# Ordering merge-gate products behind attention scores in a two-layer hybrid decoder trunk

## The chip, the cores and the metric

One NeuronCore of one Trainium2 chip runs the whole program. The metric is device time in microseconds (us) of one execution; before the change it is 1164.12 us, the median of 3 runs. Lower is better.

## What is computed

The reference is a decoder trunk of two layers on 256 tokens of width 1024, all in float32. Per layer:

```python
h = rms_norm(x, norm_g[l, 0]) * (1.0 + sc1) + sh1
p = h @ w_in[l] + b_in[l]
p_rwkv, p_q, p_kv, p_gate, p_merge = jnp.split(p, IN_SPLITS, axis=-1)
...
m_a, m_b = jnp.split(jax.nn.sigmoid(p_merge), 2, axis=-1)
mix = m_a * (y_a @ w_up_rwkv[l]) + m_b * (y_b @ w_up_nsa[l])
x = x + gate_mix * (mix @ w_out[l])
h2 = rms_norm(x, norm_g[l, 1]) * (1.0 + sc2) + sh2
...
```

Between the lines shown, `y_a` comes from the recurrent heads (8 of 64 channels), `y_b` from the sparse attention (8 query heads in 2 key groups); behind them stands the mixture of 16 experts.

The change concerns `p_merge`: 2048 columns of the input projection, of which the sigmoid gates the two branches. They depend on `h` alone, on neither branch.

## The kernel before, in words

Everything lies transposed (channels on partitions, tokens along the free axis). A layer runs through these stages: input norm; projections of the recurrent heads; the recurrent branch, which for each of four pairs of heads prepares (`prep`), inverts (`inverse`) and then runs a chain of four chunks (`chain`, lines 626 to 704); the attention branch; the "up" products, where the two branches are projected and gated (lines 1077 to 1094); the output projection; routing; the experts, whose weights (about 1 MB a load, L1076) stream in through rings of buffers.

**Merge tiles.** The 2048 gate columns are done as 16 tiles of 128 columns by `merges(n)` (lines 713 to 721), which takes the next n of them each time it is called. A tile is made in four steps. ACT rounds the weights to the high half (`split`, L274), DVE makes the low half (L275), each over 128 x 1024. PE multiplies in 24 products of 128 x 256 (`mm3`, L288): for each of 8 slices of the contraction high by high, low by high and high by low. ACT takes the tanh into `mth` (L721). The two halves lie in the tags `w20` and `w21` of the pool `wsp`, which has 2 buffers for each tag, so two tiles can be held at once; the PSUM tag `mm` has 2 buffers. One 1 MB weight load (L160, `in_win`) serves two tiles and lies in a ring of 3 buffers (`ringa`), whose later users are the first three expert loads.

**Order.** The program is traced once in Python, and a list scheduler then lays out each engine's queue: what was traced earlier has priority, and what is ready sooner than its elders fills gaps. Buffers go to tiles in that order too. Each engine runs its queue strictly in the order laid out. `tc.issue_after(x)` adds the condition that what the block traces on x's engine stands behind x in that queue; nothing waits for x's result.

The recurrent and the attention work of a layer is interleaved by the list `STEPS`, which ends in "c2 c3 q1 m4 r": the last two chains, a projection, merge tiles 0 to 3, and the rotation of the queries. Behind it stands the attention proper. It first makes the zero-padded keys `KZ` (L938 on DVE, L939 on ACT), then compressed attention for two halves of the queries (L947 to L966). Then it runs over two groups g (lines 970 to 1028):

- 16 score matrices, 4 heads r for each of two query halves qt (L982, PE), which take turns in the PSUM tags `tr` and `rw`; the masked maximum of each (L985, DVE); exponentials (L991, ACT); sums and scaling (L993 to L1001, DVE);
- for hp = 0 and 1, the group's "middle": `merges(2)`, one step of the modulation vector (`ada_step`, L225 on DVE, weights by L223), transposes of the probabilities (L1012 to L1014), copies (L192, ACT), the products with the values (L1020 to L1026), and the output (L1028).

So tiles 4 to 7 are traced in group 0, 8 to 11 in group 1, and 12 to 15 behind both. The lines of the loop that the change touches:

```python
            for hp in range(2):
                merges(2)
                ada_step()
```

Of the kernel before, what the change touches and what calls it, by code (L numbers as in the profile page):

```python
# [18 lines left out]
T = 256  # L19
# [92 lines left out]
def tile_trunk(ctx: ExitStack, tc: tile.TileContext, a: dict, layers=L, dump=None):  # L112
    nc = tc.nc
    ve, ac, po, pe, sp = nc.vector, nc.scalar, nc.gpsimd, nc.tensor, nc.sync
# [17 lines left out]
    def ps(tag):  # L132
        return phase["pool"].tile([128, 512], F32, name="ps_" + tag, tag=tag, bufs=phase["bufs"][tag])
# [56 lines left out]
    def cp(e, out, x):  # L190
        if e == "a":
            ac.activation(out, x, AF.Copy)  # L192
        else:
            ENG[e].tensor_copy(out, x)
# [77 lines left out]
    def split(hi, lo, x, e=ve):  # L272

        ac.activation(hi, x, AF.Copy)  # L274
        e.tensor_sub(lo, x, hi.bitcast(F32))  # L275
# [7 lines left out]
    def mm3(out, w2, x2, ks=range(NK)):  # L283

        for j in range(2):
            for k in ks:
                for i in range(2 - j):
                    pe.matmul(out, lhsT=w2[i][:, k, :], rhs=x2[j][:, k, :], start=(k == ks[0] and not (i or j)),  # L288
                              stop=(k == ks[-1] and j == 1), skip_group_check=True)
# [8 lines left out]
    with tc.tile_pool(name="start", bufs=8, reuse_waits="tile") as start:  # L298
# [11 lines left out]
        for ci in (2, 0, 3, 1):  # L310
            p = ps("mm")
            for r in range(2):
                w = load("ada0", ci, r, pool=start)
                for j in range(4):
                    pe.matmul(p[32 * j:32 * j + 32, :], lhsT=csx[:, 4 * r + j], rhs=w[:, 512 * j:512 * j + 512],
                              start=(r == 0), stop=(r == 1), skip_group_check=True)
            rows_ = start.tile([128, 512], F32, name="adar", tag="adar", bufs=2)
            ac.activation(rows_, p, AF.Copy)
            p = ps("rw")
# [8 lines left out]
    for l in range(layers):  # L328
# [8 lines left out]
        def pair(name, pool):  # L337

            return [pool.tile([128, NK, T], F32R, name=f"{name}{i}", tag=f"{name}{i}") for i in range(2)]

        h2 = pair("h2", lay)
# [6 lines left out]
        def parts(k, n):  # L348

            return [wsp.tile([128, 1024], F32R, name=f"w2{i}", tag=f"w2{i}")[:, 0:k * n].rearrange("p (k n) -> p k n", k=k)  # L350
                    for i in range(2)]
# [29 lines left out]
        def wcol(ci, l=l, win=win):  # L381
            if ci not in win:
                win[ci] = load("win", l, ci).rearrange("p (k n) -> p k n", k=4 if 8 <= ci < 12 else NK)
            return win[ci]
# [321 lines left out]
        def ada_step():  # L706

            if todo:
                ada_piece(*todo.pop(0), crow, adp)

        merged = iter(range(16))

        def merges(n):

            for j in itertools.islice(merged, n):
                w = wcol(12 + j // 2)
                p = ps("mm")
                w2 = parts(NK, 128)
                split(*w2, w[:, :, 128 * (j % 2):128 * (j % 2) + 128])
                mm3(p[:, 0:T], w2, h2)  # L720
                ac.activation(mth[:, j, :], p[:, 0:T], AF.Tanh, scale=0.5, bias=hbm[:, j:j + 1])  # L721


        def nt(shape, name, bufs=1, dt=F32, pool=None):
            return (pool or nka).tile([128] + shape, dt, name=name, tag=name, bufs=bufs)
# [18 lines left out]
        qT = nt([4, T], "qT")  # L744
# [140 lines left out]
        for step in STEPS.split():  # L885
            n = int(step[1:]) if step[1:] else 0
# [42 lines left out]
        KZ = nt([2, 2, T], "KZ")  # L929
        PcT = nt([2, T], "PcT")  # L930
        p = ps("tr")
# [12 lines left out]
        for qt in range(2):  # L944
            p = ps("tr")
            for h in range(8):
                pe.matmul(p[:, 32 * h:32 * h + 32], lhsT=qT[:, h // 2, qt * 128:qt * 128 + 128], rhs=KCZ[:, h % 2, :],  # L947
                          start=True, stop=True)
# [21 lines left out]
        for g in range(2):  # L970
            E = []
            for qt in range(2):
                n = 128 * (qt + 1)
                S_ = nt([4, 2, n], f"S{qt}", 2)
                mx = nt([4, 2], "mx", 2)
                am = R[:, C_AM + 128:C_AM + 256] if qt == 0 else R[:, C_AM:C_AM + 256]
                for r in range(4):
                    h = 4 * g + r
                    p = ps("rw" if r % 2 else "tr")
                    p3 = p[:, 0:2 * n].rearrange("p (b k) -> p b k", b=2)  # L980
                    s = slice(64 * (h % 2), 64 * (h % 2) + 64)
                    pe.matmul(p3, lhsT=qT[s, h // 2, qt * 128:qt * 128 + 128], rhs=KZ[s, g, :, 0:n],  # L982
                              start=True, stop=True)
                    for b in range(2):
                        ve.tensor_tensor_reduce(S_[:, r, b, 0:n], p3[:, b, :], am, 1.0, NEG, op0=ALU.add, op1=ALU.max,  # L985
                                                accum_out=mx[:, r, b:b + 1])
                ve.tensor_scalar(mx, mx, -0.125, None, op0=ALU.mult)
                sm_ = nt([4, 2], "sm", 2)
                for r in range(4):
                    for b in range(2):  # L990
                        ac.activation(S_[:, r, b, 0:n], S_[:, r, b, 0:n], AF.Exp, scale=0.125, bias=mx[:, r, b:b + 1],  # L991
                                      accum_out=sm_[:, r, b:b + 1])
                ve.tensor_scalar(sm_, sm_, TINY, None, op0=ALU.max)  # L993
                ve.reciprocal(sm_, sm_)
                ve.tensor_mul(sm_, sm_, GT4[:, qt, 4 * g:4 * g + 4, 1:3])
                for r in range(4):
                    for b in range(2):
                        if K["ss"] == "a" or (K["ss"] == "x" and b):
                            ac.activation(S_[:, r, b, 0:n], S_[:, r, b, 0:n], AF.Copy, scale=sm_[:, r, b:b + 1])
                        else:  # L1000
                            ve.tensor_scalar(S_[:, r, b, 0:n], S_[:, r, b, 0:n], sm_[:, r, b:b + 1], None, op0=ALU.mult)  # L1001
                E.append(S_)
            for hp in range(2):
                merges(2)
                ada_step()
                pts = []
                for i in range(2):
                    r = 2 * hp + i
                    PT = PTs[:, 768 * i:768 * i + 768].rearrange("p (b n) -> p b n", b=2)
                    for b in range(2):  # L1010
                        p = ps("rw" if b else "tr")
                        pe.transpose(p[:, 0:128], E[0][:, r, b, 0:128], ident)  # L1012
                        pe.transpose(p[:, 128:256], E[1][:, r, b, 0:128], ident)
                        pe.transpose(p[:, 256:384], E[1][:, r, b, 128:256], ident)  # L1014
                        cp("a" if b else K["pt"], PT[:, b, :], p[:, 0:384])
                    pts.append(PT)
                po_ = ps("rc")
                for b in range(2):
                    for i in range(2):
                        pe.matmul(po_[64 * i:64 * i + 64, 0:256], lhsT=VS[:, 0, b, 64 * g:64 * g + 64],  # L1020
                                  rhs=pts[i][:, b, 0:256], start=(b == 0), stop=False, skip_group_check=True)
                    for i in range(2):
                        pe.matmul(po_[64 * i:64 * i + 64, 128:256], lhsT=VS[:, 1, b, 64 * g:64 * g + 64],
                                  rhs=pts[i][:, b, 256:384], start=False, stop=False, skip_group_check=True)
                for i in range(2):
                    pe.matmul(po_[64 * i:64 * i + 64, 0:256], lhsT=VC[:, 2 * hp + i, :], rhs=PcT[:, g, :],  # L1026
                              start=False, stop=True, skip_group_check=True)
                ac.activation(ybT[:, 2 * g + hp, :], po_[:, 0:256], AF.Copy)  # L1028
# [3 lines left out]
        while todo:  # L1032
            merges(2)
            ada_step()
# [47 lines left out]
        for j in range(NK):  # L1082
            p = ps("mm")
            w2 = [wsu.tile([128, NK, 128], F32R, name=f"w2{i}", tag=f"w2{i}") for i in range(2)]
# [24 lines left out]
        for d in range(NK):  # L1109
            pe.matmul(pL[0:16, 64:65], lhsT=rw[:, 16 * d:16 * d + 16], rhs=mod[:, 24 + d:25 + d], start=(d == 0),  # L1110
                      stop=(d == NK - 1), skip_group_check=True)
# [7 lines left out]
        for d in range(NK):  # L1119
            w = wo[d // 2]  # L1120
            p = ps("mm")
            mm3(p[:, 0:T], split_w(wsu, w[:, :, (d % 2) * 128:(d % 2) * 128 + 128], po if K["olo"] and d % K["olo"] == 2 else ve), m2)
            ve.scalar_tensor_tensor(xT[:, d, :], p[:, 0:T], gmh[:, d:d + 1], xT[:, d, :], op0=ALU.mult, op1=ALU.add)
            if d % 2:
                p = ps("tr")
# [13 lines left out]
            for tt in range(2):  # L1139
                pe.matmul(pL[:, 16 * tt:16 * tt + 16], lhsT=xT[:, d, tt * 128:tt * 128 + 128], rhs=rwg[:, d, :],  # L1140
                          start=(d == 0 and tt == 0), stop=(d == NK - 1), skip_group_check=True)
# [431 lines left out]
```

## Time and profile before

| | before |
|---|---|
| median of 3 runs | 1164.12 us (1163.97 to 1164.67) |
| the profiled execution | 1167.3 us, of which the traced span is 1165.3 us |
| PE (matmul) busy | 1051.6 us, 90% of the span |
| DVE busy | 648.6 us, 56% |
| ACT busy | 401.3 us, 34% |
| POOL busy | 135.3 us, 12% |
| DMA | 328.34 MB, mean 282 GB/s |
| attention stage, layer 0 and layer 1 | about 256 to 317 us, about 820 to 877 us |

The profile is one execution. "Busy" is the time in which an engine had an instruction in work; matmuls are pipelined, so their busy times overlap and a run of them is read by its length and count. The bracket at the end of a line of the timeline is the time for which the engine stood idle before it, and whose end it then waited for. PEclk is the granted TensorE clock as a share of full speed (2.4 GHz); its two levels are 1.2 and 2.4 GHz, so 0.80 means that part of the stretch ran at the lower one.

### The profile page before, as it was taken

The page shows a single profiled execution, that of the slowest core. Times are in us where ns is not written, and L with a number is a line of the kernel's source. Part 1 is how long each engine was busy: PE and PEld are TensorE (multiplying, and loading weights), DVE is VectorE, ACT ScalarE, POOL GpSimd, SP SyncE. Part 2 cuts the span into 40 slices and gives each one's busy share as a digit, 9 for nine tenths or more (in the row PEclk, how much of TensorE's full clock was granted, in tenths as well). Part 3 has the DMA queues.
Part 4 walks back from the last instruction along what each step waited for, and adds up shares of the span by engine and source line. Part 5 has one row for each costly group of instructions (what it writes and reads, how often), then busy time and mean ns, then how long its engine had stood idle before and what let it go on. Part 6 is the DMA issues. An engine that isn't in the chain of part 4 may idle for free. (4 is left out here: it accounts for less than half of the span.)

```text
span 1165.3 us, 19659 instructions
## 1 busy us (share of the span) xinstructions
PE 1051.6 (90%) x7568; PEld 692.5 (59%) x7568; DVE 648.6 (56%) x1725; ACT 401.3 (34%) x922; POOL 135.3 (12%) x196
## 2 busy tenths in 40 slices
PE   5769999999697999899978899999999979989997
PEld 2658766887497443344437777678769843424343
DVE  1699788878684322212148987876757452312213
ACT  1644344345553111020135444343675421202010
POOL 0431222410000000000023212322000000000000
PEclk9789999999898999999998899999999989999998
DMA  9756665475479699999985475433327969999994
GB/s 380 275 170 201 207 222 195 143 253 199 150 268 420 273 420 419 421 420 420 420 331 181 148 251 188 175 127 132 108 87 293 399 274 420 420 420 419 421 420 180
DMA packets 52801, 328.34 MB, mean 282 GB/s; under 512 B 5856, under 2 KB 7520, under 8 KB 18784
## 3 DMA queue, kind: packets, MB, share of 16 engines
q1 hardware_dynamic: 52416, 326.91, 72.4%
q8 instruction: 61, 1.00, 0.3%
q14 instruction: 36, 0.29, 0.1%
q10 hardware_dynamic: 288, 0.14, 0.0%
HBM read 325.98 MB, written 1.05 MB: 281 GB/s over the span
## 5 line engine op out<-in xcount | busy, mean ns | idle before, releaser
L288 PE MATMUL ps_mm<-h,w 128*128 128x256 f32 x1824 | 270.4, 298 | 16.5 <-ACT w L274 8.1
L288 PEld LDWEIGHTS ps_mm<-h,w 128*128 128x128 f32 x1824 | 236.9, 197 | 36.0 <-issue 10.1
L275 DVE TENSOR_TENSOR w<-w,w 128x1024 fp32r<-128x1024 f32 (+2 forms) x130 | 140.0, 1080 | 16.2 <-ACT w L274 15.6
L1368 PE MATMUL ps_mm<-w,hb 128*64 128x512 f32 (+1 forms) x576 | 136.1, 604 | 6.5 <-DMA w<-in_exp 3.4
L274 ACT ACTIVATE w<-w 128x1024 fp32r<-128x1024 f32 (+2 forms) x130 | 120.2, 937 | 62.2 <-PE ps_mm L288 36.8
L1354 PE MATMUL ps_mm<-w,xeA 128*64 128x512 f32 x512 | 120.3, 595 | 0.7 <-DMA w<-in_exp 0.7
L225 DVE CUSTOM_DVE_ANT_0 wa<-wa,crow 128x1024 f32<-128x1024 f32 x80 | 98.0, 1225 | 2.0 <-DMA wa<-in_ada 1.5
L1354 PE MATMUL ps_mm<-w,xeB 128*32 128x512 f32 (+1 forms) x640 | 89.5, 595 | 7.0 <-DMA w<-in_exp 7.0
L275 DVE TENSOR_TENSOR ys<-ps_mm,ys 128x512 fp32r<-128x512 f32 x28 | 19.2, 685 | 134.9 <-ACT ys L274 134.9
L1368 PEld LDWEIGHTS ps_mm<-w,hb 128*64 128x64 f32 (+1 forms) x576 | 38.2, 125 | 82.1 <-issue 64.9
L1354 PEld LDWEIGHTS ps_mm<-w,xeA 128*64 128x64 f32 x512 | 38.7, 137 | 69.0 <-issue 64.0
L737 PE MATMUL ps_mm<-w,h 128*128 128x512 f32 (+1 forms) x288 | 77.1, 397 | 1.3 <-DVE w L275 0.9
L1308 DVE SCALAR_TENSOR_TENSOR hb<-hb,ps_mm 128x256 f32<-128x256 f32 x28 | 11.6, 416 | 94.8 <-ACT hb L1307 94.8
L1354 PEld LDWEIGHTS ps_mm<-w,xeB 128*32 128x32 f32 (+1 forms) x640 | 26.6, 115 | 60.9 <-issue 46.0
L737 PEld LDWEIGHTS ps_mm<-w,h 128*128 128x128 f32 x288 | 48.7, 200 | 12.6 <-issue 2.7
L274 ACT ACTIVATE ys<-ps_mm 128x512 fp32r<-128x512 f32 x28 | 16.7, 597 | 108.7 <-PE ps_mm L1368 85.9
L1309 DVE SCALAR_TENSOR_TENSOR hb<-ps_mm,sw,hb 128x256 f32<-128x256 f32 x28 | 12.3, 479 | 74.4 <-PE ps_mm L1354 74.4
L288 PE MATMUL ps_mm<-y,w 128*128 128x256 f32 x384 | 49.7, 294 | 3.4 <-ACT w L274 3.1
L288 PEld LDWEIGHTS ps_mm<-y,w 128*128 128x128 f32 x384 | 48.9, 200 | 4.0 <-ACT w L274 4.0
L1318 ACT ACTIVATE hb<-ps_tr 128x256 f32<-128x256 f32 x28 | 9.4, 381 | 115.8 <-PE ps_tr L1316 115.6
L1330 DVE SCALAR_TENSOR_TENSOR xT<-ps_rw,gfh,xT 128x256 f32<-128x256 f32 x112 | 46.3, 475 | 1.6 <-PE ps_rw L1327 1.6
L1244 PEld LDWEIGHTS ps_rw<-OH,h 128*128 128x128 f32 x256 | 34.5, 205 | 20.4 <-issue 19.7
(457 smaller groups left out, 1518.0 us busy)
## 6 DMA issues: line engine op xcount, KB each, us to landing
w<-in_exp SPq DMA_DIRECT2D x192, 1024.0 KB, 19.8
w<-in_win SPq DMA_DIRECT2D x40, 1024.0 KB, 5.1
wa<-in_ada SPq DMA_DIRECT2D x80, 512.0 KB, 4.5
w<-in_ada SPq DMA_DIRECT2D x8, 1024.0 KB, 14.5
w<-in_cmp SPq DMA_DIRECT2D x8, 1024.0 KB, 5.5
w<-in_up SPq DMA_DIRECT2D x8, 1024.0 KB, 7.2
w<-in_out SPq DMA_DIRECT2D x8, 1024.0 KB, 5.8
row<-in_row SPq DMA_DIRECT2D x2, 780.0 KB, 6.8
```

Of the source, the lines that this page charges most:

```text
L225: ve.tensor_tensor_reduce(w, w, crow, 1.0, 0.0, op0=ALU.mult, op1=ALU.add, accum_out=mod[:, o:o + 1])
L274: ac.activation(hi, x, AF.Copy)
L275: e.tensor_sub(lo, x, hi.bitcast(F32))
L288: pe.matmul(out, lhsT=w2[i][:, k, :], rhs=x2[j][:, k, :], start=(k == ks[0] and not (i or j)), stop=(k == ks[-1] and j == 1), skip_group_c ...
L737: pe.matmul(p[tt][:, 0:n], lhsT=h2[j][:, k, tt * 128:tt * 128 + 128], rhs=w2[i][:, k - k0, :], start=(k == 0 and not (i or j)), stop=(k == ...
L1244: pe.matmul(p[:, k * 256:k * 256 + n], lhsT=h[:, tt, kk_ * 128:kk_ * 128 + 128], rhs=OH[:, tt, 0:n], start=(i == 0 and tt == 0), stop=(i = ...
L1308: ve.scalar_tensor_tensor(h[:, o], h[:, o], 1.0, p_g[:, o], op0=ALU.add, op1=ALU.mult)
L1309: ve.scalar_tensor_tensor(h[:, o], p_u[:, o], sw, h[:, o], op0=ALU.mult, op1=ALU.mult)
L1318: ac.activation(hsT[:, 2 * i:2 * i + 2].rearrange("p f s -> p (f s)"), p[:, 0:2 * parts], AF.Copy)
L1330: ve.scalar_tensor_tensor(xT[:, d, :], p[:, i * 256:i * 256 + 256], gfh[:, d:d + 1], xT[:, d, :], op0=ALU.mult, op1=ALU.add)
L1354: mm = pe.matmul(p[o:o + n, :], lhsT=xe[:, k, x:x + n], rhs=w[:, k % 4, :], start=(k == 0), stop=(k == NK - 1), skip_group_check=True)
L1368: pe.matmul(p2[n][o:o + m, :], lhsT=hsT[:, 2 * r + g, o:o + m], rhs=w[:, g, n * 512:n * 512 + 512], start=(r + g == 0), stop=(r + g == 2), ...
```

## The change

In both groups and both layers, the products of the first pair of merge tiles of the middle (hp = 0: tiles 4 and 5 in group 0, 8 and 9 in group 1) are put behind the last score matmul of that group on PE. The splits of their weights on ACT and DVE and the tanh carry no such condition. The pair at hp = 1 and the tiles behind both groups are traced as before.

```diff
-        def merges(n):
+        def merges(n, after=None):
 
             for j in itertools.islice(merged, n):
                 w = wcol(12 + j // 2)
                 p = ps("mm")
                 w2 = parts(NK, 128)
                 split(*w2, w[:, :, 128 * (j % 2):128 * (j % 2) + 128])
-                mm3(p[:, 0:T], w2, h2)
+                if after:
+                    with tc.issue_after(after.ins):
+                        mm3(p[:, 0:T], w2, h2)
+                else:
+                    mm3(p[:, 0:T], w2, h2)
                 ac.activation(mth[:, j, :], p[:, 0:T], AF.Tanh, scale=0.5, bias=hbm[:, j:j + 1])
...
-                    pe.matmul(p3, lhsT=qT[s, h // 2, qt * 128:qt * 128 + 128], rhs=KZ[s, g, :, 0:n],
-                              start=True, stop=True)
+                    mm = pe.matmul(p3, lhsT=qT[s, h // 2, qt * 128:qt * 128 + 128], rhs=KZ[s, g, :, 0:n],
+                                   start=True, stop=True)
...
             for hp in range(2):
-                merges(2)
+                merges(2, None if hp else mm)
                 ada_step()
```

## Rows read from the trace of the kernel before

**Rows 1.** Stretches: length; PE, PEld, DVE, ACT, POOL busy (instructions); clock; DMA share; GB/s.

```profile
225.30:275.00 49.70, 47.75 (x349) 40.09 (x348) 38.94 (x103) 23.27 (x52) 5.68 (x7) 1.00 0.62 212
275.00:316.80 41.80, 29.64 (x209) 22.27 (x209) 29.19 (x116) 24.32 (x82) 0.00 (x0) 0.88 0.46 154
295.90:304.60 8.70, 1.11 (x6) 0.74 (x5) 8.56 (x37) 6.54 (x30) 0.00 (x0) 0.80 0.19 60
316.80:342.50 25.70, 25.56 (x200) 25.35 (x201) 21.68 (x48) 13.14 (x24) 0.00 (x0) 0.93 0.71 277
380.00:400.00 20.00, 20.00 (x97) 10.08 (x98) 9.37 (x31) 4.79 (x10) 0.00 (x0) 0.93 0.53 205
420.00:560.00 140.00, 132.90 (x783) 54.09 (x779) 32.25 (x79) 18.69 (x42) 0.00 (x0) 1.00 1.01 420
797.50:839.50 42.00, 40.34 (x296) 33.56 (x294) 29.84 (x90) 20.93 (x49) 3.66 (x7) 1.00 0.36 126
839.50:876.60 37.10, 32.74 (x263) 25.89 (x263) 20.65 (x92) 26.20 (x84) 0.00 (x0) 1.00 0.29 102
876.60:902.00 25.40, 25.23 (x197) 25.02 (x198) 21.36 (x46) 12.83 (x24) 0.00 (x0) 0.93 0.71 274
```

**Rows 2.** The same view of line 288 alone: length, PE busy (products), PEld busy.

```profile
225.30:275.00 49.70, 33.35 (x241) 29.59 (x240) 1.00 0.62 212
275.00:316.80 41.80, 7.89 (x48) 7.28 (x48) 0.88 0.46 154
797.50:839.50 42.00, 26.51 (x188) 23.24 (x188) 1.00 0.36 126
839.50:876.60 37.10, 13.80 (x102) 12.64 (x102) 1.00 0.29 102
```

**Rows 3.** Timeline of PE, layer 0, last score of group 0 to "up".

```profile
273.65 1.09 PE L982 MATMUL ps_tr<-KZ,qT 64*128 64x512 f32 x2
...
301.04 0.42 PE L1012 MATMUL ps_tr<-C,S 128*128 128x128 f32 x1 [5.14 <-DVE S L1001]
...
304.57 0.48 PE L1013 MATMUL ps_tr<-C,S 128*128 128x128 f32 x1 [2.46 <-DVE S L1001]
...
314.05 0.55 PE L1110 MATMUL ps_rc<-mod,rw 128*16 128x1 f32 x16 [0.47 <-ACT ybT L1028]
```

**Rows 4.** Timeline of PE, layer 1.

```profile
811.16 5.10 PE L288 MATMUL ps_mm<-h,w 128*128 128x256 f32 x40
...
838.33 1.12 PE L982 MATMUL ps_tr<-KZ,qT 64*128 64x512 f32 x2
...
861.82 0.30 PE L1012 MATMUL ps_tr<-C,S 128*128 128x128 f32 x1 [1.37 <-DVE S L1001]
...
876.63 23.58 PE L288 MATMUL ps_mm<-y,w 128*128 128x256 f32 x180 [1.54 <-ACT w L274]
```

**Rows 5.** Timeline of ACT, layer 0: tanh of tiles 3 and 4, splits behind them.

```profile
225.33 0.47 ACT L721 ACTIVATE mth<-ps_mm,hbm 128x256 f32<-128x256 f32 x1 [0.79 <-PE ps_mm L288]
225.70 1.05 ACT L274 ACTIVATE w<-w 128x1024 fp32r<-128x1024 f32 x1
...
234.43 0.47 ACT L721 ACTIVATE mth<-ps_mm,hbm 128x256 f32<-128x256 f32 x1 [0.43 <-PE ps_mm L288]
234.80 1.05 ACT L274 ACTIVATE w<-w 128x1024 fp32r<-128x1024 f32 x1
```

**Rows 6.** Timeline of PE, layer 0, a link of the last chain.

```profile
233.55 1.90 PE L288 MATMUL ps_mm<-h,w 128*128 128x256 f32 x14
235.38 0.43 PE L657 MATMUL ps_rc<-RB,TTd 128*64 128x128 f32 x2
```

**Rows 7.** Timeline of DVE, layer 0: what that link waits for; a split between softmax steps.

```profile
234.03 0.23 DVE L655 TENSOR_SCALAR RB<-ps_sq 64x64 f32<-64x64 f32 x1 [0.79 <-ACT RB L654]
...
260.05 1.22 DVE L275 TENSOR_TENSOR w<-w,w 128x1024 fp32r<-128x1024 f32 x1
261.19 0.20 DVE L960 RECIPROCAL csm<-csm 128x8 f32<-128x8 f32 x1
```

## The prediction, made blind

> **What bounds the kernel now.** I read the table of stretches first, then line 288 alone in the same stretches, then the timeline of each engine between the last chain of the recurrent branch and the "up" products.
>
> The expert stage is bound by DMA (share 1.01, 420 GB/s over 140 us), the stages before it are not (shares 0.29 to 0.62) [rows 1]. Between them lies the stretch that the change touches, and there the reader should ask what PE does. In layer 0 from 225.3, where tile 3 ends, to 275.0, where group 0's last score ends, PE is busy 47.75 of 49.7 us; from there to the "up" products at 316.8 only 29.64 of 41.8. In layer 1 the same two stretches show 40.34 of 42.0 and 32.74 of 37.1 [rows 1]. So PE is full while the chain and group 0's scores run. What fills it are the merge tiles: 241 of the 288 products of tiles 4 to 15 stand before the last score in layer 0, 188 in layer 1, and 33.35 and 26.51 us of PE's busy time are theirs [rows 2]. The other work of PE there, 14.4 and 13.8 us, is the links of chains (recurrence, norms, softmax of the compressed attention), which wait for DVE, ACT and POOL at each step. The holes come later: in layer 0 PE waits 5.14 and 2.46 us for the probabilities of group 1, with no merge tile left to do [rows 3]. In layer 1 the same wait is 1.37 us, since two tiles were left for it [rows 4].
>
> **What the change does to the order.** It names four tiles per layer, but it holds more. Tiles 4 and 5 are split as soon as tiles 2 and 3 give up their buffers, and their products may then not start before the last score of group 0. The pool has two buffers for each half, and both are held by tiles 4 and 5. The trace shows what that means for the next: the split that follows tile 3's tanh at 225.33 starts at 225.70, and the next one not before tile 4's products are through and its tanh runs at 234.43: it starts at 234.80 [rows 5]. So tile 6 can't be split while 4 and 5 are held, nor any behind it. All of tiles 4 to 15 fall behind group 0's last score, and tiles 10 to 15, once 8 and 9 hold the buffers, behind group 1's. The other instructions of these tiles, splits and tanhs, move with the products. The condition is one of order and adds no wait of its own: on PE the held pair stands behind the last score, and group 0's transposes behind the pair. They wait for the softmax anyway, for longer than the pair's 6 us (from 295.9 to 301.04 in group 1 [rows 1, 3], and until 304.57 for the second half). The weight loads move too: each waits in SP's queue until a pair is split. That queue also carries the modulation weights, expert loads and "up" loads; I cost this at nothing, since the DMA engines have room there (shares 0.62, 0.46 and 0.36, 0.29 [rows 1]). If an "up" load were queued behind one of them, "up" would start late by that wait; this is in the upper end of the range.
>
> **The sum, part by part.**
>
> Moved work. A product in a full run takes about 0.125 us (40 in 5.10 us [rows 4]). Layer 0: 241 x 0.125 = 30.1 us now come after the last score; layer 1: 188 x 0.125 = 23.5 us [rows 2].
>
> What the chain gets back. With the tiles gone, the links of the chain no longer stand behind them. Example on PE: L655 on DVE is done at 234.26, yet L657, which needs it, starts at 235.38, after 14 merge products [rows 6, 7]: 1.1 us. Example on DVE: a split of 1.22 us runs between two steps of the compressed softmax, L960 starting at 261.19 behind it [rows 7]. Reading the links one by one from the end of tile 3 to the last score and adding only what an L288, L275 or L274 puts in front of a link, I get 10.3 us in layer 0 (6.3 on PE, 4.0 on DVE) and 9.9 in layer 1 (4.7 and 5.2). The examples are two of some 14 such places a layer. Lower end: half of it, 5, if other work takes the gaps in those queues. Upper end: 16 and 11.5, if the modulation sums (L225, about 1.1 us each, five on links in layer 0 and two smaller ones in layer 1) get out of the way as well. I take the middle, since it is what the timeline shows.
>
> The clock in the emptied stretch. With 14.4 us of PE work in some 40, the stretch resembles the hole at 295.9, where the granted clock is 0.80, more than the full one, where it is 1.00 [rows 1]. A transpose took 0.42 us behind that hole and 0.30 behind the smaller one of layer 1 [rows 3, 4], so at the lower level this work is 1.4 times as long: 0.4 x 14.4 = 5.8 us, of which I count half on the chain, 2.9. A mean clock of 0.80 is 40% of the time at the lower level: 1.2 us (layer 1: 1.1). Ends: 0 and 2.9. The Trainium skill, "TensorE: Matmul & The Clock Gate", part 1, says that the throttled clock is the default and that activity releases it; by that the whole emptied stretch would run at 1.2 GHz, which makes the sum 3.4 us larger over both layers. No row here shows the chain with the tiles taken out.
>
> The holes behind the last score. Layer 1 from 839.5 to 876.6: 37.1 us, less 102 products (12.8) and PE's idle 4.4 (37.1 - 32.74), leaves 20.0 for the attention's own work [rows 1, 2]. The same 20.0 and 48 products (6.0) in layer 0's 41.8 leave 15.8 of idle time and slow clock. With 12 tiles (36 us) behind group 0's last score there is work for nearly all of it: 8 and 9 and more in the softmax of group 1, 12 to 15 while the "up" weights land. Only the wait for ybT, 0.5 [rows 3], stays. Saved: 15.3 and 3.9. Upper end of the cost: 4 us a layer come back, because a tile's split and tanh (1.05 + 0.47 on ACT [rows 5]) now stand among the exponentials, and the probabilities come later than the two tiles behind which they hide.
>
> The "up" products. They run 25.7 us at a mean clock of 0.93 in both layers [rows 1], so 14% of them, 3.6 us, at half speed. Entered from full work, they save half of that, 1.8 a layer; lower end 0.
>
> Layer 0: 30.1 - 10.3 + 1.2 - 15.3 - 1.8 = **+3.9**. Layer 1: 23.5 - 9.9 + 1.1 - 3.9 - 1.8 = **+9.0**. Together +12.9. Everything behind "up" (output projection, routing, experts) starts that much later, and the expert stage can't catch up, as its first loads wait for buffers that the "up" stage frees. The profiled execution took 1167.3 us (span 1165.3 and 2.0 around it), 3.2 above the median of 1164.1; it would take 1180.2, and the median becomes **1177.0**.
>
> **The rivals.**
>
> Faster: only the four named tiles wait, and the others flow past them. Then the chain stays filled, tiles 8 and 9 (48 x 0.125 = 6.0 us) lie in layer 0's hole of 5.14 + 2.46, and layer 1's 1.4 is filled: about -7.4, so 1156.7. It hangs on whether tile 6 finds a buffer for its split while 4 and 5 hold theirs. For it: the holes are there. Against it: the split that waits for the tile two before it [rows 5]. A stronger return of the chain would lead to the same side only if the last score came earlier by more than (30.1 + 23.5 - 15.3 - 3.9 - 3.6) / 2 = 15.4 us a layer on the mean, against the 10.1 read off. Chance 0.07.
>
> No change: the expert stage absorbs it. If its end is set by when its loads begin, and the first three ring buffers, the slots of the merge weights, are filled well before, a later "up" costs nothing: 1164.1. For it: the share of 1.01. Against it: DMA is at 0.53 from 380 to 400 [rows 1], with its buffers full and waiting for the first expert products, so those products set the pace from there on. Chance 0.06.
>
> Slower still: the emptied stretch runs wholly at the lower clock and the chain gets back only half. Over both layers 3.4 us more for the clock and 10.2 for the chain: +13.6 on the sum, 1190.6. It decides if group 0's last score of layer 0, which ends at 274.7 now, ends no earlier than about 272. For it: the links are short and the gaps between them long. Against it: rows 6 and 7, where the cause of the delay is in plain sight. Chance 0.15.
>
> **How the numbers follow.** The forecast has 0.72. Its own bounds: all favourable ends together (16 and 11.5 back, no clock cost) give -3.0 + 6.3, some +3, 1167; the holes coming back by 4 us a layer give +21, 1185. The range reaches on to the third rival and a little past it, 1167 to 1193; it leaves out the faster case, no change, and a remainder of the slowest, together under 0.2. Chances, with 0.2% (2.3 us, about what a measurement of this kernel can tell from no change) as the bound: slower 0.72 + 0.15, same 0.06, faster 0.07.
>
> **What would show it.** In the changed profile: no product of L288 from "h" between tile 3's tanh and group 0's last score, in both layers; that score some 9 us earlier (near 266 in layer 0, and near 834 in layer 1, which itself begins 4 us later); then PE nearly without idle time to the "up" products, group 1's wait for probabilities gone in layer 0; "up" beginning some 6 us later in layer 0 and 11 in layer 1, counted from tile 3, and running at a clock near 1.00. Merge products among the chain would prove me wrong on the buffers; a last score no earlier would move the sum to the third rival; a hole of several us after group 1's last score would add to it.

## The result and the profile after

The changed kernel takes **1198.63 us** (median of 4 runs, 1193.75 to 1204.99) against 1164.39 for the kernel before in the same comparison: ratio 1.0268, interval 1.0226 to 1.0311. The prediction had the sign right and 1177.0 with a range of 1167 to 1193, so the time lies outside. The profiled execution took 1197.61 us (span 1195.7), 30.3 more than that of before.

First the stretches, cut at the same events as in [rows 1]: tile 3's end, group 0's last score, the start and the end of "up". Layer 1's first stretch is cut once more, at its first score. Columns as in [rows 1].

```profile
225.20:270.10 44.90, 28.93 (x151) 19.72 (x151) 30.06 (x96) 11.83 (x34) 5.52 (x7) 0.70 0.43 141
270.10:327.00 56.90, 50.84 (x391) 43.50 (x391) 40.27 (x125) 36.54 (x100) 0.00 (x0) 0.97 0.59 211
...
806.30:827.90 21.60, 10.20 (x76) 7.46 (x74) 12.52 (x35) 5.69 (x15) 3.87 (x7) 0.65 0.29 98
827.90:853.30 25.40, 25.40 (x74) 16.77 (x74) 10.89 (x49) 6.87 (x23) 0.00 (x0) 0.50 0.00 1
853.30:908.20 54.90, 51.48 (x396) 45.02 (x396) 30.55 (x101) 35.51 (x95) 0.00 (x0) 0.96 0.40 152
```

The last column but two is the granted clock. Before, it was 1.00 from tile 3 to group 0's last score in both layers [rows 1]. Now it is 0.70 in layer 0; in layer 1 it is 0.65 up to the first score and 0.50 through all the scores, although PE counts as busy for the whole 25.40 us. The same stretch from first to last score took 17.9 us before (821.58 to 839.45; its end is in [rows 4]). PE's timeline of before, at its start:

```profile
821.58 1.13 PE L982 MATMUL ps_rw<-KZ,qT 64*128 64x256 f32 x4 [0.32 <-ACT KZ L939]
```

Line 288 alone in the same stretches, as [rows 2]:

```profile
225.20:270.10 44.90, 7.66 (x43) 6.42 (x43) 0.70 0.43 141
270.10:327.00 56.90, 30.97 (x246) 29.72 (x247) 0.97 0.59 211
...
806.30:853.30 47.00, 10.34 (x41) 8.50 (x39) 0.57 0.14 45
853.30:908.20 54.90, 33.63 (x251) 32.13 (x252) 0.96 0.40 152
```

So 198 and 147 products have moved behind the last score, as against the 241 and 188 foretold. The missing ones are the held tiles 4 and 5, most of whose products still stand in front of it. The timeline of PE in layer 1 shows where:

```profile
824.20 0.69 PE L696 MATMUL ps_rc<-C,adx 128*128 128x128 f32 x2 [5.15 <-DVE adx L693]
827.88 5.81 PE L986 MATMUL ps_rw<-KZ,qT 64*128 64x256 f32 x8 [2.99 <-ACT KZ L943]
833.62 1.86 PE L288 MATMUL ps_mm<-h,w 128*128 128x256 f32 x7
...
835.70 3.46 PE L951 MATMUL ps_tr<-KCZ,qT 128*128 128x32 f32 x16
...
840.31 1.22 PE L986 MATMUL ps_tr<-KZ,qT 64*128 64x256 f32 x2
841.46 2.07 PE L288 MATMUL ps_mm<-h,w 128*128 128x256 f32 x8
...
851.27 2.07 PE L986 MATMUL ps_tr<-KZ,qT 64*128 64x512 f32 x2
853.27 2.07 PE L288 MATMUL ps_mm<-h,w 128*128 128x256 f32 x8
```

The score behind which the change holds the tiles (second query half, r = 3) writes to a PSUM tile of tag "rw". It is the last in the program, but in PE's queue the eight "rw" matmuls go first, at 827.88, and the scores of tag "tr" follow one after the other, the last at 851.27. The hold ends at 833.6, and the held products mix with the "tr" scores. At the low clock eight of them take 2.07 us, twice what they take in a full run [rows 4].

The buffers behave as the prediction read them. The timeline of ACT in layer 0, beside [rows 5]:

```profile
225.18 0.47 ACT L725 ACTIVATE mth<-ps_mm,hbm 128x256 f32<-128x256 f32 x1 [0.77 <-PE ps_mm L288]
225.55 1.05 ACT L274 ACTIVATE w<-w 128x1024 fp32r<-128x1024 f32 x1
...
264.58 0.47 ACT L725 ACTIVATE mth<-ps_mm,hbm 128x256 f32<-128x256 f32 x1 [0.35 <-PE ps_mm L288]
264.95 1.05 ACT L274 ACTIVATE w<-w 128x1024 fp32r<-128x1024 f32 x1
```

Between the split behind tile 3's tanh and the next split of a merge tile lie 39.4 us, against 9.1 before. The next split is tile 6's, and it waits for tile 4's buffer.

At the other end, between group 1's last score and "up" in layer 1:

```profile
875.92 5.94 PE L288 MATMUL ps_mm<-h,w 128*128 128x256 f32 x48
883.52 0.33 PE L1017 MATMUL ps_tr<-C,S 128*128 128x128 f32 x1 [1.23 <-DVE S L1005]
...
887.64 5.83 PE L288 MATMUL ps_mm<-h,w 128*128 128x256 f32 x47
...
896.67 11.72 PE L288 MATMUL ps_mm<-h,w 128*128 128x256 f32 x96
...
908.23 22.88 PE L288 MATMUL ps_mm<-y,w 128*128 128x256 f32 x192
```

Tiles 8 and 9 stand in front of group 1's transposes, 10 and 11 between its halves, and 12 to 15 alone in front of "up". "up" itself takes 22.88 us, against 25.01 before (876.63 to 901.64), and its row shows the clock at 1.00:

```profile
908.20:931.10 22.90, 22.90 (x196) 22.77 (x195) 18.74 (x41) 11.40 (x21) 0.00 (x0) 1.00 0.61 237
```

Counted from the end of tile 3's tanh, "up" ends 124.2 us later in layer 0 (116.0 before) and 124.1 later in layer 1 (103.6 before). That is **+8.2 and +20.4**, 28.6 of the 30.3 us; the steps had +3.9 and +9.0.

### The profile page after: what moved, and what is told of

It is laid out like the page before. It is cut to its first block, busy times and chain, and to the rows that moved or that the text cites. A ratio compares the mean times of both kernels' runs of the same rounds, so it can differ in the third digit from the quotient of the medians.

```text
span 1195.7 us, 19648 instructions
## 1 busy us (share of the span) xinstructions
PE 1066.1 (89%) x7568; PEld 699.1 (58%) x7568; DVE 650.3 (54%) x1725; ACT 400.9 (34%) x922; POOL 135.0 (11%) x196
## 5 line engine op out<-in xcount | busy, mean ns | idle before, releaser
L1334 DVE SCALAR_TENSOR_TENSOR xT<-ps_rw,gfh,xT 128x256 f32<-128x256 f32 x112 | 46.3, 475 | 1.6 <-PE ps_rw L1331 1.6
L1248 PEld LDWEIGHTS ps_rw<-OH,h 128*128 128x128 f32 x256 | 34.8, 207 | 20.6 <-issue 18.9
L288 PE MATMUL ps_mm<-y,w 128*128 128x256 f32 x384 | 45.8, 281 | 0.0
L288 PEld LDWEIGHTS ps_mm<-y,w 128*128 128x128 f32 x384 | 45.6, 188 | 0.0
```

Source lines behind the costliest of these rows:

```text
L1248: pe.matmul(p[:, k * 256:k * 256 + n], lhsT=h[:, tt, kk_ * 128:kk_ * 128 + 128], rhs=OH[:, tt, 0:n], start=(i == 0 and tt == 0), stop=(i = ...
L1334: ve.scalar_tensor_tensor(xT[:, d, :], p[:, i * 256:i * 256 + 256], gfh[:, d:d + 1], xT[:, d, :], op0=ALU.mult, op1=ALU.add)
```

## The experiments

**Theories.** A: the two pinned weight buffers push twelve tiles behind group 0, that is, work is moved. Clock: the stretch that this empties falls to the low clock, and the scores with it. B: the held products mixed among the scores are the loss. C: the second group's hold carries a large part of it. Times of layer events are given in us from the end of tile 3's tanh, in the profiled execution. This leaves out the start of the program, in which that end moves between 224.6 and 233.0 in layer 0 from run to run with no change to the code there. Each row of times is of one execution; of the first score and of "up" it gives the start, of the last score the end.

| kernel | ratio to before (95%) | layer 0: first score, group 0's last, "up" | layer 1: the same |
|---|---|---|---|
| before | 1 | 30.8, 48.9, 91.0 | 23.6, 41.4, 78.6 |
| the change | 1.0268 (1.0226 to 1.0311) | 25.0, 44.5, 101.3 | 20.8, 46.3, 101.2 |
| e1 last in the queue | 1.0286 (1.0238 to 1.0334) | 25.0, 45.6, 104.3 | 20.6, 40.0, 96.3 |
| e2 group 0 alone | 1.0243 (1.0200 to 1.0285) | 27.3, 47.4, 102.8 | 20.4, 45.2, 99.0 |
| e8 group 1 alone | 1.0202 (1.0143 to 1.0262) | 30.0, 50.3, 104.6 | 23.6, 43.3, 94.4 |
| e3 192 products added | 1.0215 (1.0170 to 1.0261) | 25.1, 42.7, 100.3 | 21.3, 35.9, 97.0 |
| e5 96 added | 1.0229 (1.0169 to 1.0289) | 25.1, 45.4, 104.3 | 21.2, 45.3, 99.0 |
| e9 120 added | 1.0183 (1.0145 to 1.0221) | 25.1, 44.9, 104.5 | 21.4, 36.0, 93.2 |
| e6 tiles 12 to 15 cut | 1.0170 (1.0111 to 1.0230) | 27.3, 47.4, 98.0 | 20.5, 45.1, 92.3 |
| e4 14, 15 held alone | 1.0003 (0.9980 to 1.0026) | 32.5, 50.6, 91.7 | 23.6, 41.4, 78.7 |
| e7 12 to 15 held | 0.9991 (0.9960 to 1.0021) | 31.1, 50.0, 90.4 | 23.6, 41.4, 78.6 |
| e10 before, PE kept busy | 1.0040 (1.0010 to 1.0069) | 30.6, 48.8, 92.7 | 23.5, 41.4, 80.4 |

**e1: hold behind the score that is last in PE's queue.**

```diff
                     mm = pe.matmul(p3, lhsT=qT[s, h // 2, qt * 128:qt * 128 + 128], rhs=KZ[s, g, :, 0:n],
                                    start=True, stop=True)
+                    held = mm if r == 2 else held
...
-                merges(2, None if hp else mm)
+                merges(2, None if hp else held)
```

> Edit: as the change, but tiles 4, 5 and 8, 9 are held behind the r = 2 score of the second query half, which is the last score in PE's queue in group 0 (the r = 3 score, behind which the change holds them, stands third or fourth there). Theory A (the two weight buffers are pinned, so 12 tiles pile up behind group 0, and the emptied stretch falls to the low clock; the products mixed among the scores only trade places): no held product before the last score of group 0; first to last score shrinks from 25.4 us to 15 to 18 in layer 1 and from 19.4 to 12 to 15 in layer 0, but the 43 and 41 products now come behind it, where PE is nearly full, so the time stays near the changed kernel's 1198.6: 1188 to 1202. Theory B (the loss is the 41 to 43 held products mixed among the scores at the low clock, 10.3 us in layer 1 and 7.7 in layer 0): the time falls by 13 us or more, to 1185 or less.

Measured 1202.4 us (1196.21 to 1205.55). B falls: without any held product among the scores the time is no better (layer 1's "up" comes 4.9 us earlier than in the change, layer 0's 3.0 later). But the scores did not become as quick as A expected either (first to last 19.5 us in layer 1, 20.6 in layer 0), and PE's timeline in layer 1 says why:

```profile
843.46 3.46 PE L951 MATMUL ps_tr<-KCZ,qT 128*128 128x32 f32 x16
847.44 1.22 PE L986 MATMUL ps_tr<-KZ,qT 64*128 64x256 f32 x2 [0.52 <-DVE csc L955]
849.35 1.19 PE L986 MATMUL ps_tr<-KZ,qT 64*128 64x256 f32 x2 [0.69 <-DVE mx L990]
851.31 2.04 PE L986 MATMUL ps_tr<-KZ,qT 64*128 64x512 f32 x2 [0.76 <-DVE csm L965]
```

The score matmuls alone, each waiting for what reads the one before, still take 1.2 and 2.0 us a pair. The held products cost 6 us here (25.5 less 19.5). What remains goes with the clock, in the stretch from the first to the last score:

```profile
837.20:856.70 19.50, 16.80 (x37) 8.45 (x37) 9.82 (x49) 5.62 (x21) 0.00 (x0) 0.50 0.00 1
```

**e2 and e8: one group's hold alone.** The first diff is e2 (group 0), the second e8 (group 1).

```diff
-                merges(2, None if hp else mm)
+                merges(2, None if hp or g else mm)
```

```diff
-                merges(2, None if hp else mm)
+                merges(2, mm if g and not hp else None)
```

> Edit: only the first group's tiles 4 and 5 are held; tiles 8 and 9 of the second group are free. Theory A (the pinned buffers of the first group empty the chain's stretch, everything else follows): nearly the whole loss stays, 1190 to 1200; the granted clock of the stretch up to group 0's last score stays near 0.70 and 0.57. Theory C (the second group's hold carries a large part, since it leaves 96 products alone in front of the up products): 1180 or less.

> Edit: only the second group's tiles 8 and 9 are held; 4 to 7 flow through the chain as before. Theory A (holding a middle tile pins the buffers under all later ones): tiles 8 to 15, 192 products or 24 us, stand behind group 1's last score in both layers, against about 0 and 64 before; less the holes there (7.6 and 1.4 us) and some 5 us that the chain gets back, 6 to 11 us a layer: 1176 to 1188, though the clock stays high while tiles 4 to 7 last. Rival (the second hold costs nothing, as the run with only the first group's hold was as slow as both): 1162 to 1169.

Measured 1195.3 (1189.98 to 1198.06) for e2 and 1193.0 (1190.92 to 1195.12) for e8. C falls by e2. But e8 is not free, and its loss is larger than A expected. Each hold alone costs nearly what both cost together, which fits the buffers: either hold pins both, and what comes behind the later of the two ends up in front of "up". In e8 that is 192 products behind group 1's last score. The chain keeps tiles 4 to 7, but group 0's last score comes no earlier than before: with a granted clock of 0.74 and 0.77 up to it, it comes at 50.3 and 43.3 against 48.9 and 41.4. So "up" is late by 13.6 and 15.8.

**e3, e5, e9: keep PE busy in the emptied stretch.** The diff is that of e3; e5 has 4 in place of 8, e9 has 5.

```diff
                 split(*w2, w[:, :, 128 * (j % 2):128 * (j % 2) + 128])
+                for _ in range(8 if j == 4 else 0):
+                    mm3(p[:, 0:T], w2, h2)
                 if after:
```

> Edit: as the change, and tile 4's 24 products are traced 8 more times without the hold, into the PSUM tile that its own products then overwrite: 192 products per layer are added, and nothing else differs. Theory of the clock (the emptied stretch is slow because the clock falls, not because of what stands in it): the granted clock from tile 3's end to group 0's last score rises from 0.57 to over 0.85 in layer 1 and from 0.70 to over 0.85 in layer 0, and layer 1's last score comes no later than the changed kernel's 47.0 us after tile 3, although some 100 or more products are added in front of it; the time stays within 1185 to 1200. Theory of the load (PE's queue is what delays the scores, the clock is a minor thing): 100 to 190 products of 0.125 us in front of the last score put it 12 to 24 us later, and the time goes to 1210 or more.

> Edit: as the change, with tile 4's 24 products traced 4 more times without the hold: 96 products per layer are added, all of them in front of group 0's first score; behind group 0's last score the order of PE is the changed kernel's. Clock theory (the emptied stretch loses to the low clock what the filler with 192 products gave back, and the rest of the loss is moved work in front of the up products): granted clock over 0.9 up to the last score in both layers; last score of layer 1 at 35 to 39 us after tile 3 (46.3 in the changed kernel), of layer 0 at 42 to 44 (44.5); the up products begin 54 to 57 us behind it as in the changed kernel; sum against before about +5 in layer 0 and +9 in layer 1, so 1176 to 1186. Rival (the gain of the first filler came from its order behind the last score): last score of layer 1 at 46 or later and 1195 or more.

> Edit: as the change, with tile 4's 24 products traced 5 more times without the hold (120 per layer). In layer 1 the score stretch then has PE's order of the run with 192 products, 14 of them between the first scores, and behind the last score little more than the changed kernel's own products; it differs from the run with 96 by those 14 products in the score stretch. Clock theory (the drop begins in the wait between the first scores, 0.93 us in the run with 96, and lasts to the end of the score stretch): clock 1.00 in layer 1 up to the last score, which comes at 35 to 37 us after tile 3 (45.3 with 96 products, 46.3 in the changed kernel); the up products of layer 1 begin 88 to 93 us after tile 3 (101.2 in the changed kernel, 78.6 before), so what is left, 10 to 14 us, is moved work; in all 1182 to 1192. Rival (the number of products in front of the first score decides, or the clock falls anyway): last score of layer 1 at 44 or later and 1193 or more.

Measured 1191.25 (1187.78 to 1196.57), 1196.31 (1193.61 to 1202.49) and 1188.23 (1186.24 to 1189.46). With 192 useless products more per layer the kernel is no slower than the change (its median is 7 us lower, with overlapping intervals), and layer 1's last score comes 10.3 us earlier with about 140 products in front of it. The theory of the load, by which it should have come 12 to 24 us later, falls.

The run with 96 missed what was expected, and with e9 it makes the sharpest pair. The rows below are stretches of layer 1: tile 3's end to first score, then to last score. First e5, then e9.

```profile
814.00:835.20 21.20, 19.41 (x164) 17.17 (x162) 11.87 (x33) 5.18 (x13) 4.06 (x6) 1.00 0.30 101
835.20:859.30 24.10, 23.14 (x74) 16.03 (x74) 10.95 (x50) 6.88 (x23) 0.00 (x0) 0.58 0.00 0
```

```profile
806.20:827.60 21.40, 19.73 (x167) 17.55 (x166) 12.02 (x33) 5.37 (x15) 4.10 (x6) 1.00 0.29 100
827.60:842.20 14.60, 14.60 (x80) 10.07 (x79) 9.71 (x48) 4.71 (x18) 0.00 (x0) 1.00 0.00 1
```

Up to the first score the two are alike. Then e9 has 8 products between the first four scores and the next, where PE in e5 waits 0.93 us; behind the next four it has 6 and e5 has 7. In e5 the clock falls just after that wait and stays at 0.50 until the last pair of scores: 24.1 us in all. In e9 it stays at 1.00 and more work is done in 14.6. These are single executions, but the times of the four runs of each differ the same way, without overlap. PE's timeline of e9, to be laid beside that of the changed kernel above:

```profile
827.61 1.13 PE L988 MATMUL ps_rw<-KZ,qT 64*128 64x256 f32 x4
828.66 1.21 PE L288 MATMUL ps_mm<-h,w 128*128 128x256 f32 x8
829.80 1.98 PE L988 MATMUL ps_rw<-KZ,qT 64*128 64x512 f32 x4
...
832.76 1.87 PE L953 MATMUL ps_tr<-KCZ,qT 128*128 128x32 f32 x16
...
835.23 0.70 PE L988 MATMUL ps_tr<-KZ,qT 64*128 64x256 f32 x2
835.85 1.21 PE L288 MATMUL ps_mm<-h,w 128*128 128x256 f32 x8
...
841.11 1.12 PE L988 MATMUL ps_tr<-KZ,qT 64*128 64x512 f32 x2
```

Sixteen small products 1.87 us instead of 3.46, a pair of scores 1.12 instead of 2.07. So in layer 1 the clock alone costs the changed kernel at least 10.3 us up to the last score (46.3 against 36.0, with 120 products more in front of it). What is left at "up" in e9, 93.2 against 78.6, arises behind the last score (57.3 us from there to "up", 37.2 before), which fits moved work; 88 to 93 was expected. All that the fillers gain lies between the first and the last score: the first comes at 21.3 and 21.4 in e3 and e9 and at 20.8 in the change, where PE waits 5.15 and 2.99 us in front of it for DVE and ACT.

In layer 0 the fillers did less: the clock from first to last score was still 0.83 in e9 and 1.00 only in e3, where the last score came 1.8 us earlier than in the change. That is less than what executions differ by there. In e2 and e6 PE's order up to that score is the change's, and the score came 2.9 us later (47.4 against 44.5). The clock fell sooner in them, as the first sixteen small products show; PE's timeline of the change, then of e6:

```profile
230.03 1.87 PE L951 MATMUL ps_tr<-KCZ,qT 128*128 128x32 f32 x16
```

```profile
234.66 3.46 PE L953 MATMUL ps_tr<-KCZ,qT 128*128 128x32 f32 x16
```

In e9 "up" of layer 0 comes 3.2 later than in the change. Half of that arises where group 1's second transposes and products with the values take 5.5 us at a granted clock of 0.69, in the change 4.0 at 1.00; no run tells why the clock falls there.

**e6: leave out the work in front of "up".**

```diff
-                else:
+                elif j < 12:
                     mm3(p[:, 0:T], w2, h2)
+                else:
+                    pe.matmul(p[:, 0:T], lhsT=w2[0][:, 0, :], rhs=h2[0][:, 0, :], start=True, stop=True)
```

> Edit: as the change, but tiles 12 to 15, which stand alone in front of the up products, do one of their 24 products each: 92 products per layer are left out of the computation. Theory of moved work (these products lie on the path, 0.125 us each): the up products begin 10 to 12 us earlier in each layer than in the changed kernel, 1173 to 1180. Rival (the start of the up products is set by their weights or by group 1's probabilities, and the products only fill that wait): under 5 us a layer, 1189 to 1199.

Measured 1189.21 (1187.21 to 1192.12): between theory and rival, nearer to the rival. "up" begins 3.3 and 8.9 us earlier than in the change, and ends 0.1 later and 4.7 earlier. Layer 0 had lost 2.9 us to the clock before; counted from group 0's last score, "up" begins 6.2 and 7.7 us earlier and ends 2.8 and 3.5 earlier. PE's timeline in layer 1:

```profile
897.82 0.39 PE L726 MATMUL ps_mm<-h,w 128*128 128x256 f32 x1 [0.56 <-ACT w L274]
899.66 10.89 PE L288 MATMUL ps_mm<-y,w 128*128 128x256 f32 x62 [1.46 <-ACT w L274]
911.03 15.65 PE L288 MATMUL ps_mm<-y,w 128*128 128x256 f32 x130 [0.48 <-DVE w L275]
```

"up" now waits for its own weights to be split (the releaser is the split on ACT) and takes 26.3 and 27.0 us instead of 22.9. In layer 1 its loads are issued at 892.47, 85.1 us after tile 3, and in the change at 87.5; before at 73.2. So of the 11.5 us of products cut (92 x 0.125), some 8 had been hiding the landing and splitting of the "up" weights, which are themselves issued late.

**e4 and e7: hold tiles under which no earlier tile waits.** A table of held tiles by number takes the place of the argument; shown is e7. In e4 nothing is held behind group 0 and r is 3.

```diff
-                if after:
-                    with tc.issue_after(after.ins):
+                if j in hold:
+                    with tc.issue_after(hold[j].ins):
...
+                    held = mm if r == (3 if g else 2) else held
...
+            hold.update({j: held for j in ((12, 13), (14, 15))[g]})
...
-                merges(2, None if hp else mm)
+                merges(2)
```

> Edit: tiles 4 to 13 are free as in the kernel before, only tiles 14 and 15 are held, behind group 1's last score. No later tile waits for their buffers. In layer 1 the order hardly differs from before; in layer 0 48 products move from in front of group 1's scores to behind them, into the waits for group 1's probabilities (5.14 and 2.46 us before). Theory A (holding as such costs nothing, pinning buffers under later tiles does): 1156 to 1162, layer 0's up products 3 to 7 us earlier. Rival (the probabilities are late for DVE and ACT, so that the waits only shift): 1163 to 1166.

> Edit: no tile is held that pins buffers which an earlier tile needs: 12 and 13 are held behind the last score in PE's queue of group 0, 14 and 15 behind group 1's. In layer 1 the order is the one before; in layer 0 48 products leave the score stretch of group 0, and tiles 14 and 15 stand behind group 1's scores. Theory A (work moved into holes is a gain): 1158 to 1163, layer 0's up products 3 to 6 us earlier than before. Rival (as with the last two tiles alone: scores and probabilities are set by DVE and ACT, the holes shift): 1163 to 1168.

Measured 1166.95 (12 runs, 1163.24 to 1172.18; before 1166.96) and 1165.15 (12 runs, 1162.76 to 1174.53; before 1166.14): no difference. Holding four tiles behind the two last scores costs nothing when no other tile needs their buffers. Nor does it gain anything. In e7 PE's timeline of layer 0 has tiles 14 and 15 in the holes:

```profile
297.14 4.41 PE L288 MATMUL ps_mm<-h,w 128*128 128x256 f32 x35
302.37 0.30 PE L1018 MATMUL ps_tr<-C,S 128*128 128x128 f32 x1 [0.82 <-DVE S L1006]
...
306.12 0.33 PE L1019 MATMUL ps_tr<-C,S 128*128 128x128 f32 x1 [1.44 <-DVE S L1006]
```

The waits of 5.14 and 2.46 us [rows 3] are down to 0.82 and 1.44, but the transposes come no earlier (76.0 and 79.8 us after tile 3, before 75.2 and 78.8): group 1's probabilities are ready when DVE and ACT have made them. The hole was room, not time.

**e10: the kernel before, with PE kept busy in front of "up".**

```diff
         merges(16)
+        warm = ps("mm")
+        with tc.issue_after(av.ins):
+            for i in range(24):
+                pe.matmul(warm[:, 0:T], lhsT=h2[0][:, 0, 0:128], rhs=h2[0][:, i % NK, :], start=True, stop=True)
```

Here `av` is group 1's last product with the compressed values.

> Edit: the kernel before, and 24 products per layer of stored operands into a PSUM tile that nobody reads, held behind group 1's last product with the compressed values, in the wait in front of the up products. It adds work and leaves nothing out. Theory (the up products lose 2 us a layer to the low clock because PE waits some 2.4 us in front of them, and run 22.9 us when entered from full work): up products 22.9 to 24 us instead of 25.0, starting at most 0.5 later, 1 to 4 us less in all: 1160 to 1165 where the kernel before gives 1166. Rival (the up products wait for their weights, or lose the clock further in): 1165 to 1168, up products 25 us.

Measured 1170.62 (12 runs, 1166.26 to 1179.35; before 1164.97): slower by 0.4%, where a gain was expected. Its "up" stretches in both layers:

```profile
322.30:346.80 24.50, 23.84 (x194) 23.21 (x195) 21.19 (x45) 12.44 (x23) 0.00 (x0) 1.00 0.65 249
...
880.40:906.50 26.10, 25.40 (x194) 24.77 (x195) 21.09 (x45) 12.37 (x24) 0.00 (x0) 0.93 0.61 234
```

In layer 0 the clock is now 1.00, and "up" still takes 24.5 us, since its weights are late: a split on ACT still waits for their load when "up" has already begun.

```profile
323.67 1.15 ACT L274 ACTIVATE w<-w 128x512 fp32r<-128x512 f32 x2 [0.88 <-DMA w<-in_up]
```

In layer 1 the clock is 0.93 as before. "up" begins 1.7 and 1.8 us later. No version tried here beats the kernel before.

## Why the prediction was right on the sign and wrong on the size

**What the change does to the order: right on the buffers, wrong on one word.** All of tiles 6 to 15 waited for the two buffers, as [rows 5] said, and e4 and e7 show that without that wait the hold is free. But "group 0's last score" was taken to be the one that the code names last. In PE's queue that one is third or fourth of eight, so tiles 4 and 5 did not fall behind the last score. I had the rows for it: the last score in [rows 3, 4] is of tag "tr", and the code's r = 3 writes to "rw". By e1 this cost 6 us in layer 1's scores and nothing in the time. The wait that was to cover the held pair was misread too: 5.14 us is less than the pair's 6. In layer 1 of the changed kernel group 0's first transposes follow held products without a wait (857.66), but the second ones still wait 1.60 us for their probabilities.

**Moved work and holes: right as a sum, in part by luck.** From the last score to "up" the steps gave +14.8 (30.1 - 15.3) and +19.6 (23.5 - 3.9); measured +14.8 and +17.7. But only 198 and 147 products moved, at 0.125 each 24.8 and 18.4 us, so the holes gave back 10.0 and 0.7 us, not 15.3 and 3.9: two misses that cancel. As a reading it was too simple: e6 shows that with the last products gone the "up" weights set the start, and e7 that a hole filled is not by itself time saved.

**The clock: the step that failed.** It read "at the lower level this work is 1.4 times as long: 0.4 x 14.4 = 5.8 us, of which I count half on the chain, 2.9", then took 40% of that, 1.2 and 1.1 us. Three things were off. The 1.4 came from two single transposes; the rows of after and e9 give 3.46 / 1.87 and 2.07 / 1.12, both 1.85. The granted clock was taken as 0.80, that of the hole at 295.9; it was 0.70 and 0.57. And of the scores not half but all lies on the chain (25.4 us against 14.6 in e9). In layer 1 the term measures at least 10.3 us instead of 1.1. Some 5 of these are the held products' own, which by the forecast would not have stood there: 41 of them take 10.34 us, and 41 x 0.125 is 5.1. For the links alone e1 gives an estimate: 16.8 us of PE work at the low clock, 7.7 us less when divided by 1.85. In layer 0 e3 gives 1.8 us for the forecast's 1.2, but executions of one order differ there by 2.9, so its size in layer 0 stays open.

The prediction set this against the Trainium skill, "TensorE: Matmul & The Clock Gate", part 1: throttled by default, released by activity. For this stretch that was nearer the mark than the 0.80: 0.50 through layer 1's scores. But the 3.4 us for it went by the same 1.4 and the same half.

**What the chain gets back: not settled.** 10.3 and 9.9 were foretold. The last score came 4.4 us earlier in layer 0 and 4.9 later in layer 1. With the clock held up it came 5.4 to 6.2 earlier (e9 and e3 in layer 1, e3 in layer 0). That is a lower bound, with filler and held products in the chain's way: 44 of them in e9's scores, where PE is busy for all of 14.60 us. No run has the chain alone at the high clock. An estimate from e1 in layer 1: 19.5 us less the 7.7 above leaves 11.8 for the scores, if the waits between them stay as they are, against 17.9 before; with the first score 3.0 us earlier that makes 9.1, near the 9.9.

**"up": right in size (-2.1 a layer for -1.8), in part for another reason.** [rows 1] show it at 0.93 before and it ran at 1.00, but e10 shows that at 1.00 it still needs 24.5 us when its weights are only just in. In layer 1 of the changed kernel they had been loading since 894.53, 13.7 us before.

**The account.** Layer 0: the last score was foretold 9.1 earlier and came 4.4 earlier, which is the +4.3 by which the layer's end was missed (8.2 for 3.9) within half a us; how much of it is the clock's is open, as said. Layer 1: foretold 8.8 earlier, it came 4.9 later, 13.7 us, of which the next stretch gave back 1.9 and "up" 0.3: 11.5, against 11.4 missed (20.4 for 9.0). Of the 13.7, at least 9.2 are the clock (10.3 for 1.1).

**The rivals.** "Faster" fell by the split at 264.95, "no change" by the end of the span, which is as late as layer 1's "up". "Slower still" was the nearest, and is not what happened either: its sign was a last score of layer 0 no earlier than 272, it came at 270.2, and its clock cost 3.4 us over both layers, where layer 1 alone had at least 9.2 more than the forecast. A range whose upper end had all 14.4 and 13.8 us of links at twice their length would have held the time.

## What to carry to other kernels

An order condition on a piece of work also holds its buffers: ask what the next user of each buffer is, and look up in the engine's queue, not in the code, where the named instruction stands. Before emptying a stretch of PE, price everything that stays in it at the low clock, 1.85 times as long here, and count all of it where each step waits for the one before on PE. Work that fills the gaps of a chain can be worth more than the gaps it causes: 120 useless products made the changed kernel faster.

## What the chip showed that I had not expected

The granted clock in the scores depended on how PE entered them. In e5 a wait of 0.93 us after full work was followed by 0.50 for some 20 us, with PE counted as busy throughout (23.14 of 24.1 us for the whole stretch); in e9 the same instructions with 8 products in place of that wait ran at 1.00 to the end. In layer 0 one order of instructions lost the clock at different points in different executions (the change against e2 and e6). In the changed kernel PE was busy 25.40 of 25.40 us at 0.50. "Busy" in the rows counts an instruction from start to modelled end, so it doesn't tell how full the array was; these scores use 64 rows of it. The Trainium skill, "TensorE: Matmul & The Clock Gate", part 1, has activity release the throttle; here a busy row by itself did not, and the measurement decides. What in the mix of work keeps the clock, and whether the wait itself or the missing products made it fall, no run here separates.
